# Attention's scaling moved to ScalarE one block behind, and a fifth prepared weight step for the output projection, in a one-core gated linear attention and MLP kernel

## The chip, the cores and the metric

The kernel runs on one core of one Trainium2 chip. The metric is device time in microseconds: 1041.84 us is the median of three runs of the kernel before (1041.79 to 1042.16). Engines are called by the profile's names: PE is TensorE's matmul and PEld its weight load, DVE is VectorE, ACT is ScalarE, POOL is GpSimd, SP is SyncE, which issues most of the DMAs. L797 means line 797 of the kernel before.

## The reference

For one sequence of 256 tokens of width 2048 it computes, in float32, one layer of chunk-causal gated linear attention and a squared-ReLU MLP, each behind an RMSNorm and with a residual, and a final RMSNorm:

```python
def _gla_mixer(h, w_in, w_gate_up, b_gate, o_norm, w_out):
    proj = h @ w_in                                   # q, k (1024 each), v, r (2048 each), g_low (16)
    log_a = jax.nn.log_sigmoid((g_low @ w_gate_up + b_gate).astype(jnp.float32)) / GLA_GATE_TEMP
    ...                                               # 4 heads, chunks of 64 tokens
    def step(state, xs):
        q_c, k_c, v_c, d_c = xs
        state = d_c[..., None] * state + jnp.einsum('bhck,bhcv->bhkv', k_c, v_c)
        return state, jnp.einsum('bhck,bhkv->bhcv', q_c, state)
    ...
    o = o * lax.rsqrt(jnp.mean(o * o, axis=-1, keepdims=True) + EPS) * o_norm.astype(jnp.float32)
    return (o * jax.nn.silu(r)) @ w_out

def _sq_relu_mlp(h, w_up, w_down):
    a = jax.nn.relu(h @ w_up)
    return (a * a) @ w_down

h = h + _gla_mixer(_rmsnorm(h, gla_norm), ...)
h = h + _sq_relu_mlp(_rmsnorm(h, mlp_norm), w_up, w_down)
return _rmsnorm(h, final_norm)
```

The change touches how `o` is normalised (the `rsqrt` of its mean square, per token and head) and how `(o * silu(r)) @ w_out` is multiplied.

## The kernel before, in words

**Precision.** Every float32 operand of a matmul is split into a high part (a cast, on ACT, L123) and a low part (the difference, on DVE, L136 or L365), and a product is three matmuls: high by high, high by low, low by high. One matmul here is a 128x128 stationary block by 256 moving columns.

**Weights.** They stream from HBM. SP's queue loads a raw tile (one of six buffers, `raw`), ACT casts it into `hi`, DVE subtracts into `lo` (five buffers each, taken in turn), TensorE multiplies. So at most some five weight tiles are ready ahead of TensorE.

**Block sums.** `group` (L294) runs one 512-column group of a matrix in eight steps, one for each pair of 128-row blocks. A step outside the set `summed` is 4 products of 6 matmuls, 24 in all. A step in `summed` forms a 2x2 block product from seven products instead of eight, 21 matmuls: 9 from the raw blocks, and 12 from sums of blocks (`weight_sums`, L233 and L234) that run one step later (`pending`, L359). A DMA on POOL's queue (L335) adds one raw block to another on the way in. At the end of a group the two banks of the sums are copied out by ACT and combined by DVE (`combine`), and the result is put in place (`put`).

**Prepared steps.** For a few steps of the output projection, `make_sums` (L242) does the sums early: it loads the pair of `w_out` blocks, forms the sums on DVE (L252, L233, L234), casts on ACT (L255), subtracts on DVE (L259) and writes both halves, 512 KB each, to HBM by POOL's queue (L256, L260). Later `group` reads them into `pre` (L330) instead of summing, casting and subtracting. There are four such steps: (group, pair) of `MADE_OUT`, L237. `MADE_AT` gives the place inside each host stage: the two halves of q, the first group of v (steps 5 and 6), the wide stage of r (steps 10 and 11). Output group 3 takes four pairs by sums (`FORMED`), groups 1 and 2 three (L960).

**Order of the stages around the change.** k and q; then four groups `x_group`: v's second half in two groups (L776, L777), the gate r's first half in two groups (L807, L808); then the rest of r (`natural`, L912); then the output projection in four groups (L953, L960). The calls in `between` run after a given step of a group: attention's scores go into the first group of v (`two_scores`, steps 1 and 4), the eight blocks `attend(hd, t)` (4 heads by 2 halves of the tokens) into the two groups of the gate: six after steps 1 to 6 of the first, two after steps 0 and 1 of the second. Each of `attend`'s blocks takes one of two PSUM banks in turn (`aux_bank`), with 6 matmuls for the first half of the tokens and 12 for the second. Then ACT squares the bank and sums (L793), DVE forms the mean (L794), POOL raises it to the power -1/2 (`rsqrt`, L521), and DVE scales the bank into `on` by two columns, `r1k` and `rs` (L797). `r1k` is the norm of the token times the query's scale.

**Who sets the order.** The program gives each engine one queue in order. A planner (a list scheduler with a model of costs) chooses the order within it from readiness in its model and from program order; `tc.issue_after(i)` fixes that what is in its block stands behind instruction `i` on the same engine, without a wait at run time of its own. `last_hi`, `last_lo`, `last_sum`, `last_end` hold the instructions that are used so.

**Displaced copies.** `xe_gt` holds copies of the first half of the tokens of blocks 5 and 6 of x, stored at another offset than the rest of x (`xA`, `xE`). `row_x` (L431) takes them as the stationary operand. `rows_of` names the steps of a group whose first product uses such a copy, and `FIRST` (L768) the order of the products in that step: with `{2: FIRST[2]}` the step of pair 2 starts with block 5, first half of the tokens. The groups at L776, L777 and L807 have it, the one at L808 has not.

## Time and profile before

| what | value |
|---|---|
| median of 3 runs | 1041.84 us (1041.79 to 1042.16) |
| the profiled execution's own time | 1041.46 us |
| its span, first to last instruction | 1039.7 us |
| granted TensorE clock, mean over the span | 0.999 |
| instructions | 23382, of them 9016 matmuls |
| bytes moved by DMA | 240.17 MB, mean 231 GB/s |

The profile's page gives each engine's busy time and share of the span. The chain of waits follows the execution back from its last instruction, at each step to what released it. The view in order of time gives start, duration, engine, line, operation and operands, with a count where like instructions follow one another, and in brackets idle time and what ended it. The view by windows gives each engine's busy time and count in a stretch. Matmuls overlap: one is recorded as about 276 ns long, while the next starts some 113 ns later, so that TensorE's pace is read from the starts, or from a count over a length, and not from durations.

### The profile page before, as it was taken

To read this page: it belongs to the slowest core of one execution; us is meant where nothing else is said; L and a number is where in the kernel's file an instruction comes from. 1 tells how busy PE (TensorE), PEld (TensorE's weight loads), DVE (VectorE), ACT (ScalarE), POOL (GpSimd) and SP (SyncE) were. 2 spreads that over 40 slices of the span, in tenths; PEclk is the share of its full clock that TensorE was granted. 3 is DMA by queue.
4 is the path that set the end of the run, shared out by engine and by line. 5 is a ranking of instruction groups with operands and counts; after the bars stand their busy time and mean duration, and the time that the engine had idled before them with its cause. 6 is when DMAs were issued, how large, how long until landed. Compare 5 with 4: busy or idle time off the path is not lost.

```text
span 1039.7 us, 23382 instructions
## 1 busy us (share of the span) xinstructions
PE 1031.1 (99%) x9016; PEld 1030.6 (99%) x9016; DVE 904.9 (87%) x1257; ACT 754.7 (73%) x1132; POOL 134.4 (13%) x181
## 2 busy tenths in 40 slices
PE   9999999999999999999999999999999999999997
PEld 9999999999999999999999999999999999999997
DVE  7769769898698776989999999999999999999887
ACT  7775546766477655678779788778778778778685
POOL 0000111210100001011111111111211111111100
PEclk9999999999999999999999999999999999999999
DMA  9967867758878776678888888887878888887772
GB/s 337 336 192 216 263 178 228 222 159 300 260 228 272 241 246 198 184 216 230 230 238 228 230 239 223 243 232 223 248 227 229 239 226 228 240 236 217 230 248 83
DMA packets 128751, 240.17 MB, mean 231 GB/s; under 512 B 11472, under 2 KB 30160, under 8 KB 128512
## 3 DMA queue, kind: packets, MB, share of 16 engines
q1 hardware_dynamic: 107472, 215.32, 64.4%
q0 software_dynamic: 20448, 21.77, 12.4%
q8 instruction: 70, 1.15, 0.4%
q10 hardware_dynamic: 720, 1.60, 0.4%
q14 instruction: 41, 0.34, 0.1%
HBM read 232.35 MB, written 6.29 MB: 230 GB/s over the span
## 4 chain that ended last, share of the span: by engine, by line
PE 98%; issue 1%; DVE 0%; ACT 0%; POOL 0%; POOLq 0%; DVEq 0%; ACTq 0%
PE up L1023 34%; PE acc L1023 28%; PE acc L305 16%; PE acc L181 10%; PE acc L224 6%; PE aux L224 2%; PE aux L181 1%; PE aux L845 1%; PE aux L696 1%; PE aux L399 0%; ACT sqf L1362 0%; PE acc L595 0%; POOL ors L521 0%; DVE on L797 0%; DVE hf L1434 0%
## 5 line engine op out<-in xcount | busy, mean ns | idle before, releaser
L123 ACT CAST hi<-raw 128x512 fp32r<-128x512 f32 (+4 forms) x656 | 518.5, 821 | 199.9 <-DVE raw L233 64.2
L136 DVE TENSOR_TENSOR lo<-raw,hi 128x768 fp32r<-128x768 f32 (+4 forms) x228 | 233.0, 1031 | 56.1 <-ACT hi L123 52.5
L1023 PE MATMUL acc<-hi,act 128*128 128x256 f32 x1696 | 247.7, 276 | 0.0
L1023 PE MATMUL up<-hh,hi 128*128 128x256 f32 x1024 | 238.7, 276 | 0.0
L1023 PE MATMUL up<-hl,hi 128*128 128x256 f32 x1024 | 238.7, 276 | 0.0
L1023 PEld LDWEIGHTS acc<-hi,act 128*128 128x128 f32 x1696 | 217.6, 188 | 0.0
L170 DVE TENSOR_TENSOR lo<-raw,hi 128x1024 fp32r<-128x1024 f32 x160 | 194.5, 1219 | 22.2 <-ACT hi L123 21.1
L1023 PEld LDWEIGHTS up<-hh,hi 128*128 128x128 f32 x1024 | 192.3, 188 | 0.0
L1023 PEld LDWEIGHTS up<-hl,hi 128*128 128x128 f32 x1024 | 192.3, 188 | 0.0
L1233 POOL DMA_DIRECT2D raw<-in_w_down x112 | 97.1, 867 | 519.3 <-DMA raw<-in_w_down 246.3
L1293 DVE TENSOR_TENSOR lo<-raw,hi 128x1024 fp32r<-128x1024 f32 x112 | 136.4, 1218 | 1.1 <-ACT hi L123 1.1
L1023 PE MATMUL up<-hh,lo 128*128 128x256 f32 x1024 | 137.0, 276 | 0.0
L1023 PE MATMUL acc<-lo,act 128*128 128x256 f32 x848 | 133.9, 276 | 0.0
L1023 PEld LDWEIGHTS up<-hh,lo 128*128 128x128 f32 x1024 | 125.7, 188 | 0.0
L1023 PEld LDWEIGHTS acc<-lo,act 128*128 128x128 f32 x848 | 113.4, 188 | 0.0
L234 DVE TENSOR_TENSOR raw<-raw 128x512 f32<-128x512 f32 x138 | 95.2, 690 | 3.3
L233 DVE TENSOR_TENSOR raw<-raw 128x256 f32<-128x256 f32 x138 | 58.3, 422 | 9.1 <-DMA raw<-in_w_out 6.1
L181 PE MATMUL acc<-hi,xA 128*128 128x256 f32 (+1 forms) x376 | 56.2, 282 | 0.0
L181 PEld LDWEIGHTS acc<-hi,xA 128*128 128x128 f32 x376 | 50.1, 190 | 0.0
L224 PE MATMUL acc<-xA,hi 128*128 128x256 f32 x288 | 49.2, 276 | 0.0
L224 PEld LDWEIGHTS acc<-xA,hi 128*128 128x128 f32 x288 | 43.3, 188 | 0.0
L1150 ACT COPY sums<-acc 128x512 f32<-128x512 f32 x46 | 26.8, 583 | 22.5 <-PE acc L1023 22.4
(226 smaller groups left out, 1444.1 us busy)
## 6 DMA issues: line engine op xcount, KB each, us to landing
raw<-in_w_up SPq DMA_DIRECT2D x128, 512.0 KB, 4.5
raw<-in_w_down SPq DMA_DIRECT2D x224, 256.0 KB, 4.5
raw<-in_w_in SPq DMA_DIRECT2D x68, 512.0 KB, 4.7
raw<-in_w_down POOLq DMA_DIRECT2D x112, 128.0 KB, 5.3
raw<-in_w_out SPq DMA_DIRECT2D x22, 512.0 KB, 6.2
raw<-in_w_down SPq DMA_DIRECT2D x16, 512.0 KB, 5.0
raw<-in_w_vg SPq DMA_DIRECT2D x14, 520.0 KB, 8.4
raw<-in_w_in SPq DMA_DIRECT2D x24, 256.0 KB, 4.3
```

The costliest lines, as they stand in the source:

```text
L123: last_hi[0] = nc.scalar.copy(to, raw)
L136: last_lo[0] = nc.vector.tensor_tensor(lo[:, s], raw[:, s], hi[:, s].bitcast(F32), op=ALU.subtract)
L170: last_lo[0] = nc.vector.tensor_tensor(to[1], dst, to[0].bitcast(F32), op=ALU.subtract)
L181: newest[0] = nc.tensor.matmul(o[:, m], x, w[:, m], start=first and c == 0, stop=last, skip_group_check=True).ins
L224: nc.tensor.matmul(o, u[:, i, s], m, start=kt == 0 and n == 0 and j % 2 == 0, stop=kt == KT - 1 and n == 2, skip_group_check=True,)
L233: nc.vector.tensor_tensor(u[:, 2], u[:, 0], u[:, 2], op=ALU.subtract)
L234: return nc.vector.tensor_tensor(u[:, 1::2], u[:, 1::2], u[:, 2:3].to_broadcast([P, 2, T]), op=ALU.subtract)
L305: newest[0] = nc.tensor.matmul(bank[:, o + d : o + d + T], x, w[:, d : d + T], start=(not filled or bank in sums_banks) and bank.name not ...
L1023: newest[0] = nc.tensor.matmul(o, x, w, start=first, stop=last, skip_group_check=True).ins
L1150: last_end[0] = nc.scalar.copy(to, src).ins
L1233: nc.gpsimd.dma_start(out=raw[:, :T], in_=src[:, 0, T:], accum_op=ALU.add)
L1293: last_lo[0] = nc.vector.tensor_tensor(to[1][:, :G], u, to[0][:, :G].bitcast(F32), op=ALU.subtract)
```

## The change

- Five prepared steps instead of four: (2, 6) is added, made in the first group of v in place of (3, 1), which is made in steps 4 and 5 of the second group of the gate. Output group 2 takes four pairs by sums, as group 3 does.
- The attention block's Square reads the bank without a scale. The mean adds a column `eps1` = mean square of the token x EPS x 256 instead of the constant EPS, so that the token's norm and the query's scale drop out of the result; the scaling has one factor, `rs`. It is an ACT copy with a scale instead of a DVE operation, and `attention(i)` issues it ahead of block i + 1 (the last one after step 2 of the second gate group).
- `score_ends` keeps the last score copies of ACT and DVE; after step 6 of the first group of v, `behind_scores` puts them into `last_end` and `last_sum`, so that the weight copies that follow stand behind them.
- The second group of the gate gets `{2: FIRST[2]}`.

```diff
-    MADE_OUT = ((1, 1), (2, 1), (3, 1), (3, 6))
+    MADE_OUT = ((1, 1), (2, 1), (2, 6), (3, 1), (3, 6))
     MADE_DOWN = ()
-    MADE_AT = ((2,), (4,), (5,), (10,))
+    MADE_AT = ((2,), (4,), (5,), (4,), (10,))
...
-    r1k = const.tile([P, NT], F32, name="r1k")
+    eps1 = const.tile([P, NT], F32, name="eps1")
...
-        nc.vector.tensor_scalar(r1k, r1, DK ** -0.5, None, op0=ALU.mult)
+        nc.vector.tensor_scalar(eps1, ms1, EPS * DK, None, op0=ALU.mult)
...
-            nc.scalar.activation(a_h[parts, o], b[parts, src : src + n], AF.Copy, scale=r1[parts, t : t + 1])
-            nc.vector.scalar_tensor_tensor(
+            score_ends[0] = nc.scalar.activation(a_h[parts, o], b[parts, src : src + n], AF.Copy, scale=r1[parts, t : t + 1]).ins
+            score_ends[1] = nc.vector.scalar_tensor_tensor(
                 a_l[parts, o], b[parts, src : src + n], r1[parts, t : t + 1], a_h[parts, o].bitcast(F32),
                 op0=ALU.mult, op1=ALU.subtract,
-            )
+            ).ins
...
+    score_ends = [None, None]
+
+    def behind_scores():
+        last_end[0], last_sum[0] = score_ends
...
-    now = next(make)
+    now_v = next(make)
...
-        1: lambda: two_scores(0), 4: lambda: two_scores(2),
+        1: lambda: two_scores(0), 4: lambda: two_scores(2), 6: behind_scores,
     }
-    x_group(0, 3 * KEYW, *V0, {i: lambda i=i: (between.get(i, nothing)(), now[i]()) for i in range(8)}, at_of_v(0), FIRST)
+    x_group(0, 3 * KEYW, *V0, {i: lambda i=i: (between.get(i, nothing)(), now_v[i]()) for i in range(8)}, at_of_v(0), FIRST)
...
-        nc.scalar.activation(sq, o, AF.Square, scale=r1k[:, t : t + 1], accum_out=ss)
-        nc.vector.tensor_scalar(ss, ss, 1.0 / DV, EPS, op0=ALU.mult, op1=ALU.add)
+        nc.scalar.activation(sq, o, AF.Square, accum_out=ss)
+        nc.vector.tensor_scalar(ss, ss, 1.0 / DV, eps1[:, t : t + 1], op0=ALU.mult, op1=ALU.add)
         rs = st.tile([P, 1], F32, tag="ors", name="ors")
         rsqrt(rs, ss)
-        nc.vector.tensor_scalar(on[:, t, vs], o, r1k[:, t : t + 1], rs, op0=ALU.mult, op1=ALU.mult)
-
-    attends = [lambda hd=hd, t=t: attend(hd, t) for hd in range(HEADS) for t in range(NT)]
+
+        def scaled():
+            nc.scalar.activation(on[:, t, vs], o, AF.Copy, scale=rs)
+
+        return scaled
+
+    attends = [(hd, t) for hd in range(HEADS) for t in range(NT)]
+    unscaled = []
+
+    def attention(i):
+        while unscaled:
+            unscaled.pop()()
+        if i < len(attends):
+            unscaled.append(attend(*attends[i]))
...
-    x_group(2, 4 * KEYW, *G0, {i + 1: f for i, f in enumerate(attends[:6])}, gate_x(0), {2: FIRST[2]})
-    x_group(3, 4 * KEYW + GT, *G1, {i: f for i, f in enumerate(attends[6:])}, gate_x(GT))
+    x_group(2, 4 * KEYW, *G0, {i + 1: lambda i=i: attention(i) for i in range(6)}, gate_x(0), {2: FIRST[2]})
+    now = next(make)
+    x_group(3, 4 * KEYW + GT, *G1, {i: lambda i=i: (attention(6 + i), now[i]()) for i in range(8)}, gate_x(GT), {2: FIRST[2]})
...
-        out_group(g, ORDER[1], FORMED if g == 3 else (0, 1, 7), {
+        out_group(g, ORDER[1], FORMED if g > 1 else (0, 1, 7), {
```

## The prediction

> **What bounds the kernel now.** I read the page's busy shares, then the chain of waits, then TensorE's own instructions in order of time, because a busy TensorE can still run at two paces.
>
> ```profile
> span 1039.7 us, 23382 instructions
> PE 1031.1 (99%) x9016; PEld 1030.6 (99%) x9016; DVE 904.9 (87%) x1257; ACT 754.7 (73%) x1132; POOL 134.4 (13%) x181
> ```
>
> TensorE is busy for 99% of the span. Work taken from VectorE or ScalarE gains only where one of them holds TensorE up. There is one such place in the chain, in the first group of the gate half's sums:
>
> ```profile
> 196.94 4.08 PE acc L305 x36
> ...
> 206.51 0.87 POOL ors L521
> 207.38 0.03 issue
> 207.41 0.82 DVE on L797
> ```
>
> The attention block of head 2, first half (the fifth of eight) waits for a PSUM bank. VectorE's scaling (L797) still reads it, and had itself waited for GpSimd's power (L521). TensorE's rows at that place:
>
> ```profile
> 207.89 0.28 PE L305 MATMUL acc<-lo,xA 128*128 128x256 f32 x1
> 208.27 0.51 PE L181 MATMUL aux<-vh,at 128*128 128x256 f32 x2
> ```
>
> And the stretch that follows, from the view by windows (length; busy time and count of PE, PEld, DVE, ACT, POOL; granted clock; DMA share and GB/s):
>
> ```profile
> 208.27:248.03 39.76, 39.76 (x336) 39.74 (x337) 35.90 (x50) 25.21 (x37) 4.76 (x5) 1.00 0.72 236
> ```
>
> Before the stop, 36 matmuls take 4.08 us: 113.3 ns each. The stop is 208.27 - 207.89 - 0.113 = 0.27 us. But after it 336 matmuls, up to the first transposes of the next stage at 248.03, take 39.76 us, 118.3 each, at a granted clock of 1.00. The code has as many there: 6 + 9 + 12 + 36 to the end of this group, 183 + 18 in the next, 72 of the stage behind. So the stop leaves TensorE in a **slower pace**, and it stays there with no wait shown. The same switch, the other way round, stands where the second group of v begins:
>
> ```profile
> 163.23 0.63 PE L305 MATMUL acc<-hi,xE 128*128 128x256 f32 x4
> 163.94 0.63 PE L305 MATMUL acc<-hi,xE 128*128 128x256 f32 x4
> ...
> 167.47 0.64 PE L305 MATMUL acc<-hi,xe_gt 128*128 128x256 f32 x4
> 168.18 0.62 PE L305 MATMUL acc<-hi,xA 128*128 128x256 f32 x4
> 168.86 0.62 PE L305 MATMUL acc<-hi,xA 128*128 128x256 f32 x4
> ```
>
> And where the first gate group begins:
>
> ```profile
> 188.24 0.64 PE L305 MATMUL acc<-hi,xe_gt 128*128 128x256 f32 x4
> 188.96 0.62 PE L305 MATMUL acc<-hi,xA 128*128 128x256 f32 x4
> ```
>
> Six matmuls at 163.23 take 0.71 us (118 ns each); six from the displaced copy `xe_gt` follow at 167.47; after them six take 0.68 us (113 ns). At 188.24, inside the fast pace, the same six cost 0.72 us instead of 0.68 and change nothing. So `xe_gt` in the middle of a stream restores the fast pace, and costs 0.04 us where it wasn't needed. The group at 215.9 has no such step now.
>
> **The change part by part.** *Scaling.* VectorE loses eight scalings, ScalarE gains eight, emitted one block later:
>
> ```profile
> L797 DVE TENSOR_SCALAR on<-aux,r1k,ors x8: 799/806/812, 199.2 to 226.6; 128x512 f32<-128x512 f32 x8
> L793 ACT ACTIVATE sq<-aux,r1k x8: 674/688/691, 194.7 to 222.2; 128x512 f32<-128x512 f32 x8
> ```
>
> VectorE gets back 8 x 0.81 = 6.4 us and its waits for GpSimd. ScalarE's new instruction isn't in the trace; the nearest row is its Square of the same bank and shape, 0.69, and L797's 0.81 is the upper end. I take 0.69: 5.5 us, beside TensorE. Does head 2's bank now come free by 208.0? Its chain:
>
> ```profile
> 199.92 0.69 DVE L234 TENSOR_TENSOR raw<-raw 128x512 f32<-128x512 f32 x1
> 200.52 0.81 DVE L797 TENSOR_SCALAR on<-aux,r1k,ors 128x512 f32<-128x512 f32 x1
> 200.64 2.31 ACT L123 CAST hi<-raw 128x512 fp32r<-128x512 f32 x3 [2.31 <-DVE raw L234]
> 204.78 0.40 DVE L794 TENSOR_SCALAR oss<-oss 128x1 f32<-128x1 f32 x2
> 205.90 0.89 POOL L335 DMA_DIRECT2D raw<-in_w_in  x1 [6.23 <-DVE raw L234]
> 206.51 1.38 POOL L521 TENSOR_TENSOR ors<-oss,mhalf 128x1 f32<-128x1 f32 x2
> ```
>
> ScalarE sat idle 2.31 us for VectorE's sums (L234), which stood behind a scaling; the mean (L794) and the DMA (L335) ahead of the power in GpSimd's queue came late for the same reason. Two scalings and their wait lay there: L797 at 199.19 after 1.11 us of idling for the power, and the one at 200.52, some 2.7 us in all. If only 2.0 of it reaches the power, that ends at 205.4 instead of 207.4, and ScalarE's 0.69, even half a microsecond late, is done by 206.6. So I let the stop go: **-0.27 us**. Without it the pace never falls: 336 x (118.3 - 113.3) ns = **-1.68 us**. Beside this stands a rule that speaks against counting a pace at all. The Trainium skill, SBUF — State Buffer, section Who interferes with whom, gives TensorE two independent read ports that contend with no one; by it no order of operands would change the pace, and only the stop itself would go. The rows at 163.23 and 168.86 (118 against 113 ns at the same shape) do not agree.
>
> *Smaller edits.* The Square loses its scale, the mean's constant comes from a column (L794, 0.14 us each), one column is formed in place of another before the groups: nothing, and at most a tenth of a microsecond per block on VectorE, under the same cover.
>
> *Displaced step in the second gate group* (`FIRST[2]`): **+0.04 us** if the pace is fast already; the insurance if it isn't.
>
> *Fifth prepared step.* Pair 6 of output group 2 goes from 24 matmuls to 21 (7 block products of 3): 3 x 113.3 ns = **-0.34 us**. Its loads are 384 KB and 2 x 512 KB in place of 512 KB, 0.9 MB more, on SP's queue; the prefetch has room:
>
> ```profile
> 328.80:350.40 21.60, 21.60 (x192) 21.60 (x191) 16.71 (x23) 14.46 (x24) 1.73 (x2) 1.00 0.84 263
> ```
>
> That is group 2: a DMA share of 0.84 at 263 GB/s; 0.9 MB in 21.6 us add 42 GB/s, some 0.13 of the share. The last group already carries two prepared steps, and its 180 matmuls show no stop in the chain. The step made in the first v group is another one of the same size. The new making adds, in steps 4 and 5 of the second gate group, a 512 KB load on SP's queue, two 512 KB stores on GpSimd's, a cast, and four VectorE operations:
>
> ```profile
> 153.59 0.42 DVE L252 TENSOR_TENSOR raw<-raw 128x256 f32<-128x256 f32 x1
> 155.27 1.04 ACT L255 CAST hi<-raw 128x1024 fp32r<-128x1024 f32 x1 [2.85 <-PE acc L305]
> 157.95 1.22 DVE L259 TENSOR_TENSOR lo<-raw,hi 128x1024 fp32r<-128x1024 f32 x1
> ```
>
> The cover there, from the windows and from the order of time:
>
> ```profile
> 215.88:239.72 23.84, 23.84 (x205) 23.84 (x204) 21.93 (x32) 17.34 (x26) 2.75 (x2) 1.00 0.64 196
> ```
>
> ```profile
> 228.28 1.21 DVE L136 TENSOR_TENSOR lo<-raw,hi 128x1024 fp32r<-128x1024 f32 x1
> 232.96 0.40 PE L305 MATMUL acc<-lo,xE 128*128 128x256 f32 x2
> ```
>
> VectorE: 0.42 + 0.42 + 0.69 + 1.22 = 2.75 us, less three scalings there (2.4): 21.93 becomes 22.3, of 201 matmuls x 113.3 ns = 22.8 us: full but not over. ScalarE: 17.34 + 1.04 + 3 x 0.69 = 20.5. The cover is the lead of the weights: pair 6's low half ends at 229.49 and is read at 232.96, 3.5 us. A faster TensorE takes 0.27 and 4.2% of the 24.7 us since 208.27, 1.3 in all; the new VectorE work less two scalings takes 2.75 - 1.62 = 1.1; so some 1.1 us remain. It is the thinnest place, and I cost it at nothing; without cover each microsecond counts in full.
>
> *Order after the scores* (`behind_scores`). From step 6 of the first v group, weight copies stand behind the last score copies on both engines. Queued behind them: pair 7's halves.
>
> ```profile
> 145.56 3.08 PE aux L696 x24
> ...
> 155.00 3.08 PE aux L696 x24
> ```
>
> ```profile
> 150.34 0.31 ACT L710 ACTIVATE at<-aux,r 64x64 fp32r<-64x64 f32 x1 [0.35 <-DVE at L711]
> 156.22 1.77 ACT L123 CAST hi<-raw 128x768 fp32r<-128x768 f32 x2
> 165.74 0.51 ACT L710 ACTIVATE at<-aux,r 64x64 fp32r<-64x64 f32 x2
> ```
>
> Pair 7's cast (second at 156.22) must now follow score copies that ran until 166.25. The first pair's last score copy ended at 150.65, 2.0 us after its matmuls (148.64). With as much, and 0.3 for VectorE's half, the second pair (158.08) is through at 160.4; cast 1.04 and subtraction 1.22 follow, 162.7, and TensorE reads the low half just after 163.23 + 0.47 = 163.70. One microsecond is left. Zero, with an upper end of 1 us.
>
> Sum: -0.27 - 1.68 - 0.34 + 0.04 = **-2.25 us**. The profiled execution took 1041.46 us (span and 1.8 around it), the median is 1041.84; the difference is put on the median: **1039.6 us**, 0.216% less. About 0.2% (2.08 us) is what a measurement of this kernel can tell from no change.
>
> **The rivals.**
> 1. *The stop stays, only shorter* (the change doesn't do what it says): ScalarE waits for the same power. For it: L797's wait ended with L521, not with VectorE. Against it: the 2.7 us above. Then the displaced step repairs the pace at 215.88: 336 less the 63 before it, 273 x 5 ns = 1.37; with 0.34: 1041.84 - 1.7 = **1040.1**.
> 2. *A new stop* where the lead is thin (pair 7 in the first v group, pair 6 in the second gate group): about 1 us, and half a group at the slow pace, 80 x 5 ns = 0.4: 1039.6 + 1.4 = **1041.0**.
> 3. *The pace has another cause*, something that begins near 208 and not the stop: TensorE runs at 118 ns from there on in any order, and only 0.27 + 0.34 go: **1041.2**. For it: nothing in the view names the cause of the pace. Against it: both switches stand at a stop or at `xe_gt`. The two independent ports of the page named above would leave only such a cause.
> 4. *Slower.* One row more, of the page's DMA issues:
>
> ```profile
> raw<-in_w_in SPq DMA_DIRECT2D x68, 512.0 KB, 4.7
> ```
>
> ScalarE's queue is in order, and a scaling that waits for the power holds the casts behind it. The power stands behind L335, which waits for a load, which waits for a raw buffer, freed by a subtraction, which waits for a cast. One turn is 1.05 + 1.22 + 4.7 (load) + 0.89 + 0.87 = 8.7 us against a lead of some 5; each turn costs TensorE 3.7. It decides from the point at which a cast that feeds the next load stands behind a waiting scaling. At two of the four pairs of blocks: 1041.84 + 7.4 - 0.3 = **1048.9**; at one, 1045.2.
>
> **How the numbers follow.** Forecast 0.56, own range 1039.2 to 1040.0; rivals 0.16, 0.14, 0.06, 0.08. The threshold, 1039.76, cuts the forecast's own range: I give 0.40 of its 0.56 to faster, 0.16 to same. Rivals 1 to 3 are within 0.2%; rival 4 is slower. The range takes in rivals 1 to 3 with a new stop of up to 1.5 us: 1039.1 to 1041.5; outside lie rival 4 and some 0.1 of tails.
>
> **What would show it.** Right: no wait of TensorE's on the scaling, 113.3 ns from 189 to 248, `xe_gt` at about 215.5 six matmuls long, 21 matmuls in pair 6 of group 2 with 12 from `pre`. Wrong: a wait before an attention block, or 118 ns beyond the second gate group's start; ScalarE idle for `ors` with casts behind it; a stop at pair 7 or pair 6.

## The result, and the profile after

The kernel after takes 1043.47 us in the median of 20 runs (1041.96 to 1045.62), the kernel before 1041.84 in 20 runs beside them (1039.73 to 1043.97). The ratio is 1.0019 with a 95% interval of 1.0013 to 1.0026: slower, by 1.4 to 2.7 us, where 1039.6 was forecast; at 0.19% it lies just inside the 0.2% that the prediction calls no change. The profiled execution of after took 1044.42 us, one of its longer ones. The head of its page:

```profile
span 1042.7 us, 23385 instructions
PE 1032.7 (99%) x9013; PEld 1032.0 (99%) x9013; DVE 901.4 (86%) x1253; ACT 759.5 (73%) x1141; POOL 136.5 (13%) x183
```

The 3 matmuls less are there (9013 for 9016), VectorE's busy time falls by 3.5 us, and TensorE is busy for 1.6 us more. TensorE's rows of after in order of time, at the four places that the prediction named or should have named:

```profile
163.46 0.63 PE L305 MATMUL acc<-hi,xE 128*128 128x256 f32 x4
164.60 0.51 PE L305 MATMUL acc<-lo,xE 128*128 128x256 f32 x2 [0.51 <-DVE lo L136]
...
168.48 0.64 PE L305 MATMUL acc<-hi,xe_gt 128*128 128x256 f32 x4
...
169.19 0.64 PE L305 MATMUL acc<-hi,xA 128*128 128x256 f32 x4
...
209.68 0.28 PE L305 MATMUL acc<-lo,xA 128*128 128x256 f32 x1
210.68 0.50 PE L181 MATMUL aux<-vh,at 128*128 128x256 f32 x2 [0.73 <-ACT on L804]
...
234.41 1.04 PE L862 MATMUL aux<-ident,on 128*128 128x128 f32 x8
235.20 0.48 PE L305 MATMUL acc<-lo,xE 128*128 128x256 f32 x2
...
257.46 0.38 PE L862 MATMUL aux<-ident,on 128*128 128x128 f32 x2
...
259.33 0.82 PE L862 MATMUL aux<-ident,on 128*128 128x128 f32 x6
```

Four matmuls at 163.46 should be followed by the next at 163.93; it comes at 164.60, so there is a **new stop of 0.67 us** at pair 7 of the first v group, and the displaced step at 168.48 does not bring the fast pace back (six matmuls in 0.71 us ahead of it and behind it). The **old stop** is longer: 210.68 - 209.68 - 0.11 = 0.89 us, 0.27 before. And the 16 transposes of the first turn, which stood together at 248.03 in before, are **split**: 8 in the second gate group, 2 and 6 behind the next displaced step. The same kernel's view by windows (columns as in the prediction; a count takes in 2 or 3 matmuls that were already running):

```profile
168.48:190.75 22.27, 22.27 (x192) 22.27 (x190) 20.28 (x27) 13.88 (x20) 3.41 (x4) 1.00 0.83 241
...
210.90:234.41 23.51, 23.51 (x209) 23.51 (x209) 18.11 (x29) 18.23 (x30) 5.60 (x7) 1.00 0.52 162
235.40:250.36 14.96, 14.96 (x130) 14.96 (x128) 13.93 (x20) 13.30 (x18) 0.00 (x0) 1.00 0.98 363
260.11:291.67 31.56, 31.56 (x270) 31.56 (x269) 20.79 (x26) 17.33 (x25) 4.54 (x6) 1.00 0.78 242
```

The second v group (189 matmuls, 117.8 ns each, 113.3 in before) and the stage from 260 (268 at 117.8, 113.3 in before) are slow now. The stretch from 210.9 to 234.4 is fast, although a stop stands ahead of it. Where after's execution loses its 3.0 us against before's, by the times at which TensorE reaches the same matmul (0.23 us of it lie ahead of the first place):

| place | before | after | behind by |
|---|---|---|---|
| displaced step of the second v group | 167.47 | 168.48 | 1.01 |
| displaced step of the first gate group | 188.24 | 190.03 | 1.79 |
| start of the second gate group | 215.88 | 217.93 | 2.05 |
| transposes in output group 0 | 288.96 | 291.67 | 2.71 |
| first matmul of the MLP | 372.21 | 374.95 | 2.74 |
| end of the span | 1039.7 | 1042.7 | 3.0 |

### The profile page after: what moved, and what is told of

The parts are those of the page before. It is cut to its first block, busy times and chain, and to the rows that moved or that the text cites. A ratio compares the mean times of both kernels' runs of the same rounds, so it can differ in the third digit from the quotient of the medians.

```text
span 1042.7 us, 23385 instructions
## 1 busy us (share of the span) xinstructions
PE 1032.7 (99%) x9013; PEld 1032.0 (99%) x9013; DVE 901.4 (86%) x1253; ACT 759.5 (73%) x1141; POOL 136.5 (13%) x183
## 4 chain that ended last, share of the span: by engine, by line
PE 95%; issue 1%; DVE 1%; ACT 1%; POOL 0%; DMA 0%; POOLq 0%; DVEq 0%; ACTq 0%
PE up L1040 33%; PE acc L1040 28%; PE acc L305 14%; PE acc L181 10%; PE acc L224 6%; PE aux L224 2%; PE aux L862 1%; PE aux L181 0%; ACT hi L123 0%; PE aux L399 0%; DMA raw<-in_w_in 0%; DVE lo L136 0%; PE aux L696 0%; POOL ors L521 0%; DVE raw L234 0%
## 5 line engine op out<-in xcount | busy, mean ns | idle before, releaser
L136 DVE TENSOR_TENSOR lo<-raw,hi 128x768 fp32r<-128x768 f32 (+4 forms) x228 | 232.6, 1030 | 58.7 <-ACT hi L123 53.6
L234 DVE TENSOR_TENSOR raw<-raw 128x512 f32<-128x512 f32 x139 | 95.8, 689 | 3.4
L233 DVE TENSOR_TENSOR raw<-raw 128x256 f32<-128x256 f32 x139 | 58.6, 422 | 10.8 <-DMA raw<-in_w_out 7.9
```

The costliest lines, as they stand in the source:

```text
L136: last_lo[0] = nc.vector.tensor_tensor(lo[:, s], raw[:, s], hi[:, s].bitcast(F32), op=ALU.subtract)
L233: nc.vector.tensor_tensor(u[:, 2], u[:, 0], u[:, 2], op=ALU.subtract)
L234: return nc.vector.tensor_tensor(u[:, 1::2], u[:, 1::2], u[:, 2:3].to_broadcast([P, 2, T]), op=ALU.subtract)
```

## The experiments

Each kernel ran 8 to 12 times, e13 five, beside 20 to 33 runs of the kernel before on the same chip; that kernel's medians there were 1042.08 to 1042.27 us. "Stop" below is the gap between two matmuls' starts less 0.11 us. The expectations count the slow restart behind it as well, which adds about 0.11; the idle time in a view's brackets or waits counts from a matmul's recorded end and is some 0.17 less. The rows are those of one execution of each kernel.

**One part of the change at a time.** Four kernels, each the kernel before with the part that its name gives.

e1_first:

```diff
-    x_group(3, 4 * KEYW + GT, *G1, {i: f for i, f in enumerate(attends[6:])}, gate_x(GT))
+    x_group(3, 4 * KEYW + GT, *G1, {i: f for i, f in enumerate(attends[6:])}, gate_x(GT), {2: FIRST[2]})
```

> The kernel before, with the displaced step in the second gate group alone. Every engine's order is that of before; six matmuls read the displaced copy. Theory of the prediction: the stop of 0.27 us at 208 stays and leaves the slow pace, the displaced step at 215.9 ends it, and 267 matmuls up to the transposes at 248 run at 113.3 instead of 117.8 ns: -1.2 us, ratio 0.9989. Rival (the pace has another cause, as the second group of v in the changed kernel suggests, where the displaced step at 168.5 didn't end the slow pace): 0.0 us, ratio 1.0000, 117.8 ns on both sides of the step.

Measured: 1041.71 us, ratio 0.9996 [0.9987, 1.0005]. In its profile the displaced step at 216.9 stands in a slow stretch, and the stretch stays slow up to 248.9. The edit did not repair the pace. The stop near 208, which the edit does not touch, is 0.67 us here, 0.27 in before: it differs by 0.4 between two executions of the same order.

e2_fifth:

```diff
-    MADE_OUT = ((1, 1), (2, 1), (3, 1), (3, 6))
+    MADE_OUT = ((1, 1), (2, 1), (2, 6), (3, 1), (3, 6))
...
-    MADE_AT = ((2,), (4,), (5,), (10,))
+    MADE_AT = ((2,), (4,), (5,), (4,), (10,))
...
```

> The kernel before with the fifth prepared step alone (made in steps 4 and 5 of the second gate group; scaling on VectorE as before, no displaced step there). Theory of the prediction: -0.34 us, ratio 0.9997. Theory from the two traces: the making takes the lead of pair 6 in that group, the planner fills the wait that its model sees there with the first 8 transposes of on, the other 8 slip past the displaced step of the next stage, and TensorE stays at the slow pace up to the transposes at 291: 280 matmuls x 4.5 ns = 1.3, less 0.34: +0.9 us, ratio 1.0009.

Measured: 1043.42 us, 1.0013 [1.0004, 1.0022]: slower by itself. In its profile TensorE stops 0.97 us for the low half of pair 6 of the second gate group, the thin lead of the prediction, although 8 of the transposes stand ahead of it; they are split as in after. The stop near 208 is 0.69.

e3_scale (scaling on ScalarE as in the change, nothing else):

```diff
-        nc.vector.tensor_scalar(on[:, t, vs], o, r1k[:, t : t + 1], rs, op0=ALU.mult, op1=ALU.mult)
+        def scaled():
+            nc.scalar.activation(on[:, t, vs], o, AF.Copy, scale=rs)
...
```

> The kernel before with the scaling on ScalarE one block behind alone (with the column for EPS; no fifth step, no displaced step in the second gate group, score copies not put ahead). Theory of the prediction: no stop in the first gate group, pace fast up to 248: -1.95 us, ratio 0.9981. Theory from the two traces: the scaling still waits for GpSimd's power, the stop at 208 stays and is as long as in the changed kernel (about 1.0 us); with the slow pace behind it +0.5 us, ratio 1.0005; with the fast pace behind it -1.0 us.

Measured: 1042.66 us, 1.0006 [0.9997, 1.0015]. The stop near 208 is not gone but is 1.26 us, the longest at that place, and the 336 matmuls behind it are slow.

e4_scale_behind (e3_scale and this line):

```diff
-        1: lambda: two_scores(0), 4: lambda: two_scores(2),
+        1: lambda: two_scores(0), 4: lambda: two_scores(2), 6: behind_scores,
```

> As the run before in this list (scaling on ScalarE alone), with the weight copies held behind the scores in the first v group. Theory of the prediction: no difference between the two, under 0.1 us. Theory from the two traces: pair 7's low half comes too late, a stop of 0.8 us at 163.8, and the second group of v stays at the slow pace, 183 x 4.5 ns = 0.8 us: 1.6 us above the run without it.

Measured: 1042.89 us, 1.0005 [0.9996, 1.0013], its runs in two clumps (five at 1041.2 to 1041.8, six at 1042.9 to 1044.2). The profiled run has the stop at pair 7, as after has and e3_scale has not; so the order behind the scores makes that stop. From the scores' end to the first gate group TensorE takes some 1.57 us more than in e3_scale (0.78 up to the displaced step of the second v group, 0.79 behind it, at the slow pace), in after and in e12 below as well. It reaches the gate group later, has no stop there, and runs 503 matmuls at 113.3 ns.

**Why the stop got longer.** ScalarE's, VectorE's and GpSimd's rows of after in order of time:

```profile
207.72 0.89 POOL L335 DMA_DIRECT2D raw<-in_w_in  x1 [6.44 <-DVE raw L234]
208.26 1.23 DVE L365 TENSOR_TENSOR lo<-raw,hi 128x1024 fp32r<-128x1024 f32 x1 [0.69 <-ACT hi L123]
208.33 2.09 POOL L521 TENSOR_TENSOR ors<-oss,mhalf 128x1 f32<-128x1 f32 x2
209.94 0.69 ACT L804 ACTIVATE on<-aux,ors 128x512 f32<-128x512 f32 x1 [1.71 <-POOL ors L521]
```

ScalarE idles 1.71 us for the power. The power stands behind the accumulating load (L335), as before, 17.7 us after the start of the group in both kernels: not one of the microseconds that the scaling freed on VectorE reached it. And the first of the two powers that the row joins, 0.86 us long in before, takes 1.57 here, up to 0.42 us after the end of VectorE's subtraction (L365). In before VectorE stood idle there, because its own scaling waited for that power.

Place and length can be told apart by e1 and e3_scale. In both the load comes late, 18.05 and 18.10 us after the start of the group. GpSimd's powers behind it, of e1 and then of e3_scale:

```profile
207.51 1.38 POOL L521 TENSOR_TENSOR ors<-oss,mhalf 128x1 f32<-128x1 f32 x2
```

```profile
206.65 2.65 POOL L521 TENSOR_TENSOR ors<-oss,mhalf 128x1 f32<-128x1 f32 x2
```

The first power of the two takes 0.87 us in e1 and 1.53 in e3_scale, and the stop is 0.67 and 1.26. So of the 1.26 us some 0.67 come of the place behind the load, and 0.59 came with the move of the scaling. In before and after, with the load at 17.66 and 17.69, the stops are 0.27 and 0.89: 0.62 came with the move. Two kernels take the power out of the way.

e5_no_power, on e3_scale:

```diff
-        nc.vector.tensor_scalar(ss, ss, 1.0 / DV, eps1[:, t : t + 1], op0=ALU.mult, op1=ALU.add)
         rs = st.tile([P, 1], F32, tag="ors", name="ors")
-        rsqrt(rs, ss)
+        nc.vector.tensor_scalar(rs, ss, 1.0 / DV, eps1[:, t : t + 1], op0=ALU.mult, op1=ALU.add)
```

> The kernel before with the scaling on ScalarE alone, as in e3_scale, and the power on GpSimd left out: VectorE's mean square and constant goes straight into the scaling as its factor, so that the attention's rows are scaled by another number than the reference's. Theory A (the scaling waits for the power, which stands behind the accumulating load on GpSimd's queue and lasts 1.5 us beside VectorE's subtraction instead of 0.86): the stop of TensorE in the first gate group, 1.37 us in e3_scale, falls under 0.3 us or goes; the time is then 0.5 to 1.4 us under e3_scale's, about 1041.2 to 1042.1 against 1042.1 before. Theory B (the scaling comes late because ScalarE has casts and squares ahead of it on its own queue): the stop stays at 0.8 us or more, and the time is that of e3_scale, 1042.7.

e6_power_first, on e3_scale (`powers` holds GpSimd's powers in their order, `added` counts the loads):

```diff
-                nc.gpsimd.dma_start(out=raw[:, :T], in_=src[:, 0, T:], accum_op=ALU.add)
+                with ExitStack() as order_p:
+                    if len(powers) > 6:
+                        order_p.enter_context(tc.issue_after(powers[2 * added[0] + 1]))
+                        added[0] += 1
+                    nc.gpsimd.dma_start(out=raw[:, :T], in_=src[:, 0, T:], accum_op=ALU.add)
...
```

> The kernel before with the scaling on ScalarE alone, as in e3_scale, and the powers put on GpSimd's queue ahead of the accumulating loads that stood before them (two powers ahead of each of the last three). Theory A: the first power of the pair at 208 starts when its mean square is there, some 1.3 us sooner, beside subtractions of 128x256 and 128x512 that still stretch it; the stop falls from 1.37 us to under 0.5; the accumulating load comes 1 to 2 us later, with 5 us until its rows are needed; time 1041.3 to 1042.2. Theory B: no change, 1042.7, the stop 0.8 us or more.

Measured: e5 1039.97 us, 0.9981 [0.9972, 0.9989]; e6 1040.12 us, 0.9982 [0.9974, 0.9991]. Theory A holds and B falls. Both times lie 1.2 us below the expected ranges, which had counted the stop and not the pace that comes back with it. e6's rows in order of time, and its window:

```profile
204.54 0.66 POOL L806 TENSOR_TENSOR ors<-oss,mhalf 128x1 f32<-128x1 f32 x1 [3.87 <-DVE oss L804]
205.71 0.93 POOL L806 TENSOR_TENSOR ors<-oss,mhalf 128x1 f32<-128x1 f32 x1 [0.51 <-DVE oss L804]
206.60 0.88 POOL L340 DMA_DIRECT2D raw<-in_w_in  x1
...
205.72 0.69 ACT L809 ACTIVATE on<-aux,ors 128x512 f32<-128x512 f32 x1
...
208.33 0.28 PE L306 MATMUL acc<-lo,xA 128*128 128x256 f32 x1
208.45 0.39 PE L181 MATMUL aux<-vh,at 128*128 128x256 f32 x2
```

```profile
189.41:246.53 57.12, 57.12 (x506) 57.12 (x505) 47.06 (x70) 41.97 (x67) 11.94 (x12) 1.00 0.72 222
```

The power starts 0.1 us after its mean, the scaling is over at 206.4, the attention block follows without a gap, and the 504 matmuls from 189.41 on, behind the displaced step, take 113.3 ns each. The accumulating load comes later, and TensorE doesn't wait for it.

e10_before_power_first is the kernel before with e6's edit and the scaling left on VectorE.

> The kernel before, its scaling on VectorE and all else kept, with the powers put ahead of the accumulating loads alone. Theory A (the wait at 208 is that of the power behind the load, whichever engine scales): the power ends 0.9 us sooner or more, the stop of 0.27 us goes, and the 336 matmuls behind it keep the fast pace: 1040.1 to 1040.7, like e6_power_first's 1040.1; the move of the scaling to ScalarE is then worth under 0.5 us. Theory C (the scaling has to leave VectorE, whose subtraction waits behind the power): the stop stays, 0.2 us or more, or moves to the subtraction of the summed pair; 1041.6 to 1042.4.

Measured: 1039.77 us (1039.51 to 1040.65), 0.9981 [0.9972, 0.9990], the lowest median of all kernels here. Rows of it in order of time, and its window:

```profile
206.20 1.52 DVE L802 TENSOR_SCALAR on<-aux,r1k,ors 128x512 f32<-128x512 f32 x2
...
204.54 0.56 POOL L801 TENSOR_TENSOR ors<-oss,mhalf 128x1 f32<-128x1 f32 x1 [4.11 <-DVE oss L799]
205.83 0.86 POOL L801 TENSOR_TENSOR ors<-oss,mhalf 128x1 f32<-128x1 f32 x1 [0.73 <-DVE oss L799]
```

```profile
189.48:246.61 57.13, 57.13 (x507) 57.13 (x506) 52.47 (x78) 38.20 (x59) 9.99 (x12) 1.00 0.75 231
```

Nearly the whole gain that was forecast for the scaling comes from one order on GpSimd's queue (it has 504 matmuls at 113.3 ns as well), and the move to ScalarE adds nothing that can be measured (1040.12 against 1039.77, and the intervals of the ratios overlap).

**Place or stretch?** Two kernels, on e3_scale, meant to keep VectorE off while the power runs; the second adds the line that puts the summed pair's subtraction behind a copy.

```diff
         rsqrt(rs, ss)
+        copies.append(nc.vector.tensor_scalar(ss, rs, 1.0, None, op0=ALU.mult).ins)
...
-                        with tc.issue_after(last_lo[0].ins):
+                        with tc.issue_after(copies[-2] if len(copies) == 4 else last_lo[0].ins):
...
```

> The kernel before with the scaling on ScalarE alone, as in e3_scale, the powers behind the accumulating loads as there, and one small copy on VectorE (128x1, by 1.0) of each power, from which ScalarE takes the factor: VectorE waits for the power again, as it did in the kernel before, and so runs no subtraction beside it. Theory A1 (the power is stretched by VectorE's subtractions beside it): the power at 206.5 lasts 0.86 us instead of 1.53, the scaling comes 0.5 us sooner, and the stop falls from 1.37 us to between 0.6 and 0.9; time 1042.0 to 1042.7, with a stop still there and the slow pace behind it. Theory A2 (only the place behind the load counts, the stretch is none of it): the stop stays at 1.2 us or more, and VectorE's subtraction comes later too, 1042.7 to 1043.5.

> e9_vector_waits with VectorE's subtraction of the summed pair at 206 put behind the small copy of the power, so that it does not run beside that power. In five cases so far a power beside a subtraction of two operands from SBUF ended 0.41 to 0.43 us after the subtraction's end, and with VectorE idle it ended 0.59 us after the accumulating load. Theory A1: the power ends 0.6 us after the accumulating load's end, the scaling starts at once after it if ScalarE is free, 0.5 to 0.7 us sooner against the load's end than in e3_scale (1.29 us), and the stop is under 1 us. Theory A2 (place alone): the power ends 1.2 us or more after the load's end all the same. The whole time: 1041.5 to 1042.7 by either, since a stop is left.

Measured: e9 1041.74 us, 1.0001 [0.9992, 1.0009]; e15 1042.28 us, 1.0004 [0.9996, 1.0013]. In e9 the subtraction was put ahead of the copy, the power behind the load takes 1.41 us beside it, and the stop is 1.25. In e15 the planner also put the load behind this pair of powers, so that place and length changed together: the first of them stands alone, and the stop near 208 is gone. Its time is no better than before's, because another stop came (0.65 us at 168.4, for VectorE's half of a score, L711) and 8 of the transposes stand in the second gate group; the slow pace follows both, and holds from 256 to 290 as well. Its rows show both lengths of the power within 2 us, with no load on GpSimd's queue ahead of either:

```profile
204.62 0.55 POOL L521 TENSOR_TENSOR ors<-oss,mhalf 128x1 f32<-128x1 f32 x1 [4.10 <-DVE oss L799]
206.41 1.45 POOL L521 TENSOR_TENSOR ors<-oss,mhalf 128x1 f32<-128x1 f32 x1 [1.24 <-DVE oss L802]
...
206.24 1.22 DVE L365 TENSOR_TENSOR lo<-raw,hi 128x1024 fp32r<-128x1024 f32 x1
```

With VectorE idle the power takes 0.55 us; beside the subtraction it takes 1.45 and ends at 207.86, 0.40 after it. So the stretch is there without the load, and the place behind the load costs besides, as e1 shows without the stretch.

**The transposes together.** e7_together is after with the 16 transposes fixed ahead of the displaced step of the next stage (`turn(on, ...)` behind step 2's last matmul, and the later matmuls behind the last transpose). e8_combined adds e6's edit and leaves out `behind_scores`.

> The kernel after with one thing held: the 16 transposes of the attention's first half stand together right ahead of the displaced step of the stage behind the gate groups, as they stand in the kernel before, instead of 8 in the second gate group, 2 and 6 behind the displaced step. Theory A (the split costs the pace): the displaced step sets the fast pace, and the 268 matmuls of 257 to 292 us in after run at 113.3 ns instead of 117.8, -1.2 us; against it the 8 transposes no longer fill the wait in pair 6 of the second gate group, and a stop of about 1.1 us comes there as in e2_fifth; the sum is 1043.2 to 1043.6, like after's 1043.47. Theory B (the split costs nothing, the stage behind runs at a pace of its own): the stop comes and the pace does not, 1044.3 to 1044.7. Theory C (the transposes hide nothing in pair 6): -1.2 us alone, 1042.2.

> The kernel after without the scores' place in the order of the casts (as the kernel before has it), with the powers ahead of the accumulating loads and the 16 transposes held together. If the three costs found so far are the whole of it (0.8 us at pair 7 of the first v group, some 1 us at 208, 1.2 us of slow pace from 257 to 292, less the 1.1 us stop that comes back at pair 6 of the second gate group), the time is 1043.47 - 0.8 - 0.7 - 0.1 = 1041.9, range 1041.2 to 1042.8. If the pace is set by chance at each stop, the runs spread over 1040 to 1043 and the median is the kernel before's, 1042.1.

Measured: e7 1044.52 us, 1.0023 [1.0013, 1.0033]; e8 1043.27 us, 1.0013 [1.0004, 1.0022]. TensorE's rows of e7 in order of time, and a row of the waits of e8:

```profile
249.84 1.04 PE L867 MATMUL aux<-ident,on 128*128 128x128 f32 x8
251.54 1.38 PE L867 MATMUL aux<-ident,on 128*128 128x128 f32 x8 [0.66 <-DVE on L825]
```

```profile
PE aux L873 <- DVE on L830: 2.2, 1, 2.2
```

The stage behind them runs fast in e7 (332 matmuls at 113.3 ns, Theory A's half), and no stop came at pair 6; but the second eight transposes wait for VectorE's gate product, which comes late, and the time lies in Theory B's range. In e8, whose time lies above the expected range, the stops at pair 7 and at 208 are gone; a stop of 2.3 us at the transposes (2.2 in the row) and one of 0.7 at pair 6 are left in its profile, which is that of its slowest run. Behind the first the granted clock is 0.5 for 3.4 us, with matmuls 213 ns apart, and the stage then runs slow up to 292, although its transposes stand together. So Theory A's half is not seen in e8. Both waits are for VectorE, to whose work in the second gate group the fifth step adds, and e6 and e10, without that step, have neither. So the split in after only avoided a wait that the fifth step would have brought.

**The fifth step elsewhere, and its halves.** e11 is e6 with the fifth step made in the stage behind the gate groups. The other five are e10 with one of these edits: made where the change makes it (e14), in the first v group (e13), in the second stage of the queries (e16); made and not read (e17); read and not made (e18).

```diff
-    MADE_AT = ((2,), (4,), (5,), (10,))
+    MADE_AT = ((2,), (4,), (5,), (10, 13))
...
+    MADE_AT = ((2,), (4,), (5,), (4,), (10,))
...
+    MADE_AT = ((2,), (4,), (2, 5), (10,))
...
+    MADE_AT = ((2,), (4, 8), (5,), (10,))
```

(in the order e11, e14, e13, e16)

> e6_power_first with the fifth prepared step too, made in the stage behind the gate groups (its steps 10 and 11, the fourth prepared step moved to 13 and 14) instead of in the second gate group. VectorE was busy 33.1 us and ScalarE 28.9 of the 46 us of that stage in e6_power_first, against 12.6 of 14 for VectorE in the last part of the second gate group. If the fifth step costs by its place alone, its 3 matmuls less are 0.34 us here, and the time is e6_power_first's less 0.3: 1039.5 to 1040.1. If making a step costs wherever it is made (3 loads more, 2.9 us of VectorE), 1040.5 to 1042.

> e10_before_power_first with the fifth prepared step, made in the first v group (its steps 2 and 3) instead of in the second gate group; VectorE was busy 6.6 us of the 12 from 145 to 157 us in e6_power_first. Theory A (the fifth step costs by its place): -0.34 us against e10's 1039.77, 1039.2 to 1039.8. Theory B (the making costs wherever it is: 2.9 us of VectorE, 3 loads more): 1040.5 or more.

> e10_before_power_first with the fifth prepared step made where the change makes it, steps 4 and 5 of the second gate group. Theory A (place): the stop of 0.8 to 1.1 us at pair 6 of the second gate group, and the slow pace of up to 268 matmuls behind it (1.2 us), as in e2_fifth: 1040.6 to 1042.2, 0.9 to 2.4 us over e10. Theory D (its loss in e2_fifth came of the stop at 208, which is gone here): 1039.4 to 1039.9.

> e10_before_power_first with the fifth prepared step made in the second stage of the queries, behind the second prepared step (its steps 8 and 9, at about 125 us); VectorE was busy 16.6 us of the 27 from 130 to 157 us, DMA 0.64. Theory A: 1039.2 to 1039.8. Theory B: 1040.5 or more.

> e14_fifth_gate with the fifth prepared step made but not read: output group 2 keeps its 24 matmuls at pair 6 and loads the weights as before. If the loss is the making's, the time is e14's 1040.7 plus 0.34, 1041.0 (1040.7 to 1041.5). If it lies in the use (the loads of 1.5 MB), the time is e10's, 1039.8.

> e10_before_power_first with output group 2's pair 6 multiplied as a prepared step, 21 matmuls, but with nothing made for it: it reads the prepared sums of pair 1 of the same group, so that the output is that of other weights at this pair. If the use is worth what was forecast, 1039.77 - 0.34 = 1039.4 (1039.2 to 1039.7). If the three loads more cost what the matmuls save, 1039.7 to 1040.2.

| kernel | us | ratio to before |
|---|---|---|
| e11, behind the gate groups | 1044.16 | 1.0023 [1.0014, 1.0032] |
| e13, first v group | 1045.68 | 1.0030 [1.0018, 1.0042] |
| e14, second gate group | 1040.71 | 0.9986 [0.9977, 0.9994] |
| e16, queries | 1041.17 (1039.34 to 1044.97) | 0.9997 [0.9985, 1.0008] |
| e17, made and not read | 1040.40 | 0.9980 [0.9971, 0.9989] |
| e18, read and not made | 1040.09 | 0.9980 [0.9971, 0.9989] |
| e10, without it | 1039.77 | 0.9981 [0.9972, 0.9990] |

No place makes the kernel faster than e10. Theory A, that only the place costs, falls for the places tried, though the fastest runs of e16 (1039.34) lie a little under e10's (1039.51); the change's own place is the mildest. There, what the making does to VectorE is seen in its rows of e14 and of e10, at the same part of the second gate group:

```profile
228.54 0.96 DVE L136 TENSOR_TENSOR lo<-raw,hi 128x768 fp32r<-128x768 f32 x1 [1.18 <-ACT hi L123]
229.42 1.22 DVE L259 TENSOR_TENSOR lo<-raw,hi 128x1024 fp32r<-128x1024 f32 x1
230.55 1.22 DVE L136 TENSOR_TENSOR lo<-raw,hi 128x1024 fp32r<-128x1024 f32 x1
```

```profile
226.51 2.08 DVE L136 TENSOR_TENSOR lo<-raw,hi 128x768 fp32r<-128x768 f32 x2
```

Pair 6's low half (the second L136) is ready at 231.77 in e14 and at 228.59 in e10, 3.2 us later: VectorE has the making's operations to do, and waits 1.18 us for a cast. TensorE reads it at 232.82 and 232.09, so that of 3.5 us of lead 1.05 are left, and some 0.9 of these are the 8 transposes that the planner put ahead. Behind them 133 matmuls from 232.1 to 247.8 run at 117.8 ns (0.6 us). At the other places casts wait for the made halves' stores. The waits of e16, in the window from 155 to 172 us (total, times, longest):

```profile
ACT hi L123 <- DMA made<-hi: 3.1, 1, 3.1
...
PE acc L306 <- DVE at L716: 1.1, 1, 1.1
```

The cast of a weight needs the buffer that the store to HBM still reads, waits 3.1 us, until 163.9, and TensorE later stops 1.2 us for a score's subtraction behind it. The wait alone does not make the stop: the same cast waits 2.4 us in before, 3.0 in e14 and 2.8 in e18, there until 161.5 to 162.4, and TensorE does not stop behind it. The same row has 4.8 us in e13 in that stretch, and 7.8 in e11 behind the gate groups, with a stop of 1.9 to follow. That the stores are the whole cost at these places is argued, not isolated.

e17, made and not read, came out between its two theories. Making and use can be told apart by stage, from the starts of TensorE's matmuls. From the displaced step of the first gate group to the transposes in output group 0 it takes 98.77 us in e10 and e18, 99.48 in e14 and e17: the making costs 0.71 there. From these transposes to the MLP it takes 83.62 in e10 and e17, 83.28 and 83.27 in e14 and e18: the use gains the 0.34 that was forecast. The use is seen in e10 and e18 in TensorE's rows at the start of the MLP:

```profile
371.15 0.28 PE L1029 MATMUL up<-hh,hi 128*128 128x256 f32 x1
```

```profile
370.67 0.28 PE L1029 MATMUL up<-hh,hi 128*128 128x256 f32 x1
```

e18 is ahead by 0.48 us here and near the MLP's end, 0.34 of it gained in the output projection and 0.14 before. But its span is 1038.4 against 1038.6: only 0.2 is left, because the end of the execution follows the start of the last matmul by 7.95 us instead of 7.67. Seven kernels that read the fifth step (after, e2, e7, e8, e12, e14, e18) end 7.93 to 7.96 us behind it; e11, e13 and e16, which read it too, 7.60 to 7.62; those without it 7.66 to 7.71; e17 7.26. The work in that tail is the same, and only the end of the last stores differs. Why is open.

**The change with the power first.** e12 is after, all of it, with e6's edit.

> The kernel after, all of it, with the powers ahead of the accumulating loads alone. The stop of 1.0 us at 209.7 goes; the stop of 0.8 us at pair 7 of the first v group, the thin lead of pair 6 of the second gate group and the split transposes stay: 1043.47 - 1.0 = 1042.5, range 1041.7 to 1043.2. If the stop at 209.7 was all that stood between the change and its forecast, 1040.

Measured: 1041.75 us, 0.9997 [0.9988, 1.0005]. The stop at 209.7 is gone, the stop at pair 7 (0.67 us at 163.9) and the split transposes stay: what two of the three costs leave.

## Why the prediction was wrong, point by point

By stage, after's profile loses its 3.0 us against before's so: 0.23 ahead of the displaced step of the second v group; 1.56 from there to that of the first gate group, where nothing was forecast; 0.92 from there to the transposes in output group 0, where a gain of 1.95 was forecast; 0.03 in the output projection, where before's own execution took 83.25, 0.37 less than the 83.62 of the other kernels without the fifth step; and 0.26 behind the start of the last matmul (7.94 for 7.68).

- **"So I let the stop go: -0.27 us": failed.** The step before it, "if only 2.0 of it reaches the power", was the error. The power's start is not set by its mean but by the load ahead of it in GpSimd's queue, which I had quoted with its release (`<-DVE raw L234`) and then put down to the scalings. That sum stands on VectorE behind a mean, the mean waits for the Square, and the Square for TensorE's own attention block. ScalarE's rows of before and of after:

```profile
204.21 0.69 ACT L793 ACTIVATE sq<-aux,r1k 128x512 f32<-128x512 f32 x1 [0.59 <-PE aux L181]
```

```profile
205.97 0.60 ACT L798 ACTIVATE sq<-aux 128x512 f32<-128x512 f32 x1 [0.61 <-PE aux L181]
```

  Both stand 15.9 to 16.0 us after the start of the group. Nothing reached the power, and the VectorE that was freed made it longer. Rival 1 named the wait for the power but priced the stop as shorter; it grew to 0.89 us in after and 1.26 in e3_scale. The section that I cited for TensorE's ports has a rule on exactly this: the Trainium skill, SBUF — State Buffer, Who interferes with whom, says that a VectorE instruction with two SBUF inputs contends with a GpSimd instruction that reads SBUF. The traces agree: of 48 powers in six profiles (before, after, e3, e6, e10, e15), 25 ended 0.39 to 0.42 us after the end of such an instruction, and alone the power takes 0.55 (0.84 to 0.89 as recorded right behind a load, whose row overlaps it by some 0.28).
- **"-1.68 us" of pace: the mechanism right on one condition, that the stop goes.** Where it went (e5, e6, e10) the term came: 503 or 504 matmuls at 113.3 ns up to 246 us. From the displaced step of the first gate group to the transposes in output group 0 TensorE takes 100.72 us in before and 98.77 in each of e4, e5, e6 and e10: the -0.27 - 1.68 = -1.95 us of the forecast. e6's ratio of 0.9982 is -1.9 us (-0.9 to -2.7). After takes 101.64. Of 20 profiles, 7 have a stop near 208; 5 of these are slow behind it (e9 from a stop of 0.21 us at 200.7 on), 2 are fast (after, e2). None of the 13 without it changes pace in the rest of that group. So after's -1.68 was partly gained all the same, and lost again at other stops.
- **The displaced step as "the insurance": failed.** It restores the pace at 167.47 in before, but not at 168.48 in after, nor in the second gate group of e1 and e7. I had one case for a rule, and one where nothing had to be restored. Over the 20 profiles it did so in the second v group in all 15 kernels with no stop shortly ahead of it, and in 1 of the 5 with one (in e7; not in after, e4, e12, e13); in the first gate group in 4 of the 5 that came there slow, after among them (190.03). Why is open.
- **"-0.34 us" for the fifth step: right at TensorE (83.28 for 83.62), mostly given back at the end.** **"I cost it at nothing": failed.** The step "the new VectorE work less two scalings takes 1.1; so some 1.1 us remain" was the error. Rows of after, ScalarE's and VectorE's:

```profile
229.82 1.05 ACT L255 CAST hi<-raw 128x1024 fp32r<-128x1024 f32 x1 [0.22 <-issue]
230.77 1.78 ACT L123 CAST hi<-raw 128x768 fp32r<-128x768 f32 x2
...
231.64 0.96 DVE L136 TENSOR_TENSOR lo<-raw,hi 128x768 fp32r<-128x768 f32 x1 [1.29 <-ACT hi L123]
232.51 1.22 DVE L259 TENSOR_TENSOR lo<-raw,hi 128x1024 fp32r<-128x1024 f32 x1
233.65 1.22 DVE L136 TENSOR_TENSOR lo<-raw,hi 128x1024 fp32r<-128x1024 f32 x1
```

  Pair 6's low half is ready 16.9 us after the start of the group, 13.6 in before: 3.3 us later, not 1.1. VectorE waits for ScalarE, where the scalings and the making's own cast (L255) stand ahead of the weights' casts, and I had counted ScalarE's time but not its order. TensorE came 0.6 us sooner, not 1.3. Of the lead 0.33 us is left, with 8 transposes of 0.79 us ahead of the read; without them TensorE would have stopped for some 0.46, an estimate from these times. The making also delays the product that the transposes need, which I had not followed beyond the group. That the planner then places the transposes elsewhere was in no step. By e14 against e10 the step costs some 0.9 us in the medians, in intervals that overlap; alone on the kernel before (e2) it costs 0.4 to 2.3 us.
- **"Zero, with an upper end of 1 us" for the order behind the scores: failed.** The stop of 0.67 us lies within the upper end, but with the slow pace behind it the order costs 1.57. The last score copy was taken to end at 160.4. It ended at 162.22, so the cast and the subtraction came 1.8 us later than that. Rows of after, ScalarE's and VectorE's:

```profile
160.07 0.31 ACT L710 ACTIVATE at<-aux,r 128x64 fp32r<-128x64 f32 x1 [1.41 <-DVE at L711]
...
161.91 0.31 ACT L710 ACTIVATE at<-aux,r 64x64 fp32r<-64x64 f32 x1 [0.48 <-DVE at L711]
162.24 3.99 ACT L123 CAST hi<-raw 128x1024 fp32r<-128x1024 f32 x5
...
158.19 1.22 DVE L259 TENSOR_TENSOR lo<-raw,hi 128x1024 fp32r<-128x1024 f32 x1
159.43 1.12 DVE L711 SCALAR_TENSOR_TENSOR at<-aux,r,at 128x192 fp32r<-128x192 f32 x4
...
163.32 1.22 DVE L136 TENSOR_TENSOR lo<-raw,hi 128x1024 fp32r<-128x1024 f32 x1 [0.78 <-ACT hi L123]
```

  The copies waited for VectorE's half of the scores, and that stood behind the prepared step's subtraction (L259), of the very step that is made there, with the sums L233 and L234 (0.41 and 0.67 us) between its parts. I had put 2.0 us for the second pair "with as much" as for the first, which has no prepared step beside it.
- **Rivals.** Rivals 1 and 2 came true together, where each was priced alone: stops at 209.7 and at pair 7, and at pair 6 the split transposes in place of a stop. Rival 1's stop was longer, and not shorter. Rival 3 (another cause of the pace, from 208 on in any order) falls with e5, e6 and e10. Rival 4 (a ring of waits) did not come: ScalarE waited for the power, but none of TensorE's waits in after is for a load.

## What to carry to other kernels

When an instruction is moved because it waits, look first at what stands ahead of the thing that it waits for, in that engine's queue: here one order on GpSimd gave the whole gain (1039.77 us, 0.9981 [0.9972, 0.9990]), and the move of the scaling gave none. The time freed on VectorE was taken by its next instruction, which reads two operands from SBUF and held up GpSimd's power (1.53 us for 0.87); the wait that was removed had been the cover. And a step that is "made where there is room" has to be followed to every buffer that its stores hold and to the last product of its stage, not only over the next two weight tiles.

## What the runs showed of the hardware that was not expected

- TensorE has two steady paces for the same matmuls at a granted clock of 1.00: 113.3 ns and 117.8 ns, with no wait shown. A stop often, not always, switches from one to the other (near 208 in 4 of the 6 profiles that came there fast); transposes and displaced operands among the matmuls sometimes do. The two paces over some 400 matmuls differ by 1.8 us; whether the spread of the kernel before (1039.73 to 1043.97 in 20 runs) comes of them is not shown, as one run of it was profiled. What chooses is open.
- GpSimd's power of 128x1 takes 0.55 us alone, and ends 0.39 to 0.42 us after the end of a VectorE instruction with two SBUF operands that was running when it started (1.45 us beside a 1.22 us subtraction). Beside VectorE's scaling of a PSUM bank (L797) it was not held up: in before it ends 0.33 us before that does.
- In e8 the granted clock is 0.5 for 3.4 us, from 250.7 us on, behind a stop of 2.3 us, and matmuls start 213 ns apart. None of the other profiles shows this between its first 8 and its last 8 us; their longest stop there is 1.9 us (e11).
- The end of the execution follows the start of the last matmul by 7.26 to 7.96 us, the same to some 0.05 us within a group of kernels; it changed with a prepared step made or read some 650 us earlier.
